# Poisson loss row means: longer load runs, a split first load, and partial sums folded into the last product

## The chip, the cores and the metric

The kernel runs on one core of one Trainium2 chip. The metric is the device time of one execution in microseconds (us). The time of the kernel before is the median of 12 runs.

## The reference

Two float32 arrays of 1024 rows by 4096 columns come in, and one number for each row goes out:

```python
batch, dim = 1024, 4096
loss = np.exp(log_input) - target * log_input
return np.mean(loss, axis=-1).astype(np.float32)
```

That is 33.55 MB of input, one exponential, one product and two sums for each element, and 4 KB of output.

## The kernel before

**Layout.** Partition p of the 128 holds the eight consecutive rows 8p to 8p+7 of both inputs. "Row 3" below means one row of 4096 elements on each of the 128 partitions (2 MB). `x` is `log_input`, `t` is `target`. So the work is rows 0 to 7 of x and t.

**Loads.** The list `loads` gives every transfer in order. Rows 0 to 5 come in pairs: x of two rows, then t of the same two rows, 32 KB per partition and 4 MB each. The list `TAIL` gives the rest in thirty-seconds of a row: row 6 of x and of t whole (2 MB each), and row 7 in smaller pieces, x by 24, 6 and 2, t by 12, 12, 5 and 3 thirty-seconds. All loads are issued by SP (SyncE) on one queue, line L114. The first six are moved ahead of the program's first barrier by `before_first_barrier`; nothing precedes them. The buffers `x_buf` and `t_buf` have three slots of two rows. Rows 6 and 7 reuse the slot of rows 0 and 1, so SP waits at L112 and L113, once, until two exponentials and two products are done (`exp_done`, `prod_done`), and then issues the nine loads of rows 6 and 7.

**ScalarE (ACT).** For each piece of x it computes exp into a PSUM scratch tensor, with the sum over the columns going to a column of `parts` (L139; the sum is written by a second instruction, ACTIVATION_READ_ACCUMULATOR). For each of rows 0 to 6 it also runs a small Copy over the row's two partial sums, scaled by 1/4096, whose sum is the row's loss (`join`, L123). The join of row r stands in ScalarE's order just ahead of the exp of row r + 2, for row 5 ahead of the first piece of row 7, and for row 6 after that piece. The last join, over the six partial sums of row 7 known by then, gives `most`.

**VectorE (DVE).** For each piece of t it computes -t*x with a sum over the columns (L169, again two instructions; the second is DVE_READ_ACCUMULATOR2_ANT). The pieces of t follow the loads of t. The last piece gives `rest`, already scaled. One addition of `most` and `rest` (L180) then gives row 7's loss. SP stores `all_loss`, 128 x 8, with one transfer (L185).

[...] Every load has its own semaphore (`landed`), which the engines wait for.

Of the kernel before, what the change touches and what calls it, by code (L numbers as in the profile page):

```python
# [6 lines left out]
ALU = mybir.AluOpType  # L7
F32 = mybir.dt.float32


TAIL = [
    ("x", 32), ("t", 32), ("x", 24), ("t", 12), ("t", 12), ("x", 6), ("t", 5), ("x", 2), ("t", 3),
]


def before_first_barrier(nc, instructions):

    here, first = nc.cur_bb.bb, nc.main_func.blocks[0]
    names = {i.name for i in instructions}
    here.instructions = [i for i in here.instructions if i.name not in names]
    at = next(
        k
        for k, i in enumerate(first.instructions)
        if i.engine == mybir.EngineType.SP and i.opcode == "Drain"
    )
    first.instructions = first.instructions[:at] + instructions + first.instructions[at:]  # L30


def kernel(tc, log_input, target, out):

    nc = tc.nc
    tc.close()
    tc.compile()  # L48

    P = nc.NUM_PARTITIONS  # L50
    n, d = log_input.shape
    nb = n // P
    assert nb * P == n and tuple(target.shape) == (n, d) and nb == 8 and d % 32 == 0
    inv_d = 1.0 / d
    slots = 3
    groups = nb // 2

    x_v = log_input.rearrange("(p b) d -> p (b d)", b=nb)
    t_v = target.rearrange("(p b) d -> p (b d)", b=nb)
    out_v = out.rearrange("(p b) -> p b", b=nb)  # L60


    loads = []
    for g in range(groups - 1):
        loads += [("x", 2 * d * g, 2 * d), ("t", 2 * d * g, 2 * d)]
    at = {"x": 2 * d * (groups - 1), "t": 2 * d * (groups - 1)}
    for what, w in TAIL:
        loads.append((what, at[what], w * d // 32))
        at[what] += w * d // 32
    assert at == {"x": nb * d, "t": nb * d}  # L70


    def work(kind):
        todo = []
        for i, (what, lo, w) in enumerate(loads):
            if what == kind:
                step = min(w, d)
                todo += [(a, step, i) for a in range(lo, lo + w, step)]
        return todo

    x_work, t_work = work("x"), work("t")
    n_whole = nb - 1
    assert all(w == d for _, w, _ in x_work[:n_whole] + t_work[:n_whole])

    x_buf = nc.alloc_sbuf_tensor("x_buf", [P, slots * 2 * d], F32).ap()
    t_buf = nc.alloc_sbuf_tensor("t_buf", [P, slots * 2 * d], F32).ap()
    e_dump = nc.alloc_psum_tensor("e_dump", [P, d], F32).ap()
    n_parts = len(x_work) - n_whole + len(t_work) - n_whole - 1

    parts = nc.alloc_sbuf_tensor("parts", [P, 2 * n_whole + n_parts], F32).ap()  # L90
    join_dump = nc.alloc_sbuf_tensor("join_dump", [P, 2 * n_whole + n_parts], F32).ap()
    most = nc.alloc_sbuf_tensor("most", [P, 1], F32).ap()
    rest = nc.alloc_sbuf_tensor("rest", [P, 1], F32).ap()
    all_loss = nc.alloc_sbuf_tensor("all_loss", [P, nb], F32).ap()

    def in_slot(lo, w):
        lo %= slots * 2 * d
        return slice(lo, lo + w)

    landed = [nc.alloc_semaphore(f"landed{i}") for i in range(len(loads))]  # L100
    exp_done = nc.alloc_semaphore("exp_done")
    prod_done = nc.alloc_semaphore("prod_done")
    join_done = nc.alloc_semaphore("join_done")
    loss_done = nc.alloc_semaphore("loss_done")
    out_done = nc.alloc_semaphore("out_done")


    early = []
    for i, (what, lo, w) in enumerate(loads):
        buf, src = (x_buf, x_v) if what == "x" else (t_buf, t_v)  # L110
        if lo == 2 * d * slots and what == "x":
            nc.sync.wait_ge(exp_done, 2)  # L112
            nc.sync.wait_ge(prod_done, 2)  # L113
        dma = nc.sync.dma_start(out=buf[:, in_slot(lo, w)], in_=src[:, lo : lo + w])  # L114
        dma.then_inc(landed[i], 16)
        if lo + w <= 2 * d * slots:
            early.append(dma.ins)
    before_first_barrier(nc, early)


    def join(first, count, accum, prods):
        nc.scalar.wait_ge(exp_done, exps)
        return nc.scalar.activation(  # L123
            out=join_dump[:, first : first + count],
            in_=parts[:, first : first + count],
            func=ACT_F.Copy,
            scale=inv_d,
            accum_out=accum,
        ).wait_op(prod_done, prods, "sem-ge")

    exps = 0
    for lo, w, i in x_work:
        row, col = lo // d, lo % d
        if row >= 2 and col == 0:
            join(2 * (row - 2), 2, all_loss[:, row - 2 : row - 1], row - 1).then_inc(join_done, 1)
        if col == 0 and row > 0:
            nc.scalar.wait_ge(exp_done, exps)
        k = 2 * row if row < n_whole else 2 * n_whole + exps - n_whole
        nc.scalar.activation(  # L139
            out=e_dump[:, col : col + w],  # L140
            in_=x_buf[:, in_slot(lo, w)],
            func=ACT_F.Exp,
            bias=0.0,
            scale=1.0,
            accum_out=parts[:, k : k + 1],
        ).wait_op(landed[i], 16, "sem-ge").then_inc(exp_done, 1)
        exps += 1
        if row == n_whole and col == 0:
            row -= 1
            join(2 * row, 2, all_loss[:, row : row + 1], row + 1).then_inc(join_done, 1)  # L150
    join(2 * n_whole, n_parts, most, len(t_work) - 1).then_inc(join_done, 1)


    needs = {}
    for lo, w, i in x_work:
        needs[lo + w] = i
    for j, (lo, w, i) in enumerate(t_work):
        row = lo // d
        last = j == len(t_work) - 1
        if last:  # L160
            accum = rest
        elif row < n_whole:
            accum = parts[:, 2 * row + 1 : 2 * row + 2]
        else:
            k = 2 * n_whole + len(x_work) - n_whole + j - n_whole
            accum = parts[:, k : k + 1]
        x_load = next(needs[end] for end in sorted(needs) if end >= lo + w)
        nc.vector.wait_ge(landed[x_load], 16)
        nc.vector.tensor_tensor_reduce(  # L169
            out=t_buf[:, in_slot(lo, w)],  # L170
            in0=t_buf[:, in_slot(lo, w)],
            in1=x_buf[:, in_slot(lo, w)],
            scale=-inv_d if last else -1.0,
            scalar=0.0,
            op0=ALU.mult,
            op1=ALU.add,
            accum_out=accum,
        ).wait_op(landed[i], 16, "sem-ge").then_inc(prod_done, 1)
    nc.vector.wait_ge(join_done, nb)
    nc.vector.tensor_tensor(  # L180
        out=all_loss[:, nb - 1 : nb], in0=most, in1=rest, op=ALU.add
    ).wait_op(prod_done, len(t_work), "sem-ge").then_inc(loss_done, 1)


    nc.sync.dma_start(out=out_v, in_=all_loss).wait_op(loss_done, 1, "sem-ge").then_inc(  # L185
        out_done, 16
    )
    used = landed + [exp_done, prod_done, join_done, loss_done]
    nc.sync.sem_clear(range(used[0].num, out_done.num))
    assert all(used[0].num <= s.num < out_done.num for s in used)  # L190
    nc.sync.wait_ge(out_done, 16).then_inc(out_done, -16)
# [30 lines left out]
```

## Time and profile before

| | |
|---|---|
| median of 12 runs | 84.26 us (84.18 to 84.51) |
| the profiled execution, its own time | 84.21 us |
| its span in the profile | 82.8 us |
| VectorE busy | 35.9 us (43%) |
| ScalarE busy | 33.7 us (41%) |
| DMA packets, bytes | 2304, 33.56 MB |
| product of a whole row (128x4096), VectorE | 4.42 us each, 7 of them |
| exp of a whole row (128x4096), ScalarE | 3.58 us each, 7 of them |

How to read it. The span runs from the first to the last instruction of the profiled execution; its own time includes what lies around it, 1.41 us. Busy time counts work on data; instructions that wait or issue transfers are not counted. A line of the trace in order of time gives start, duration (both us), engine, line of the kernel, operation, output and inputs, and in brackets how long the engine was idle before it and what ended that. A line of the table by stretches gives the stretch, its length, the busy time of VectorE, ScalarE and GpSimd with the number of instructions, the TensorE clock, the DMA share (packets are counted where they begin, so a short stretch can be above 1), and GB/s.

### The profile page before, as it was taken

What the parts mean: (1) busy time and instruction counts of PE and PEld (TensorE: products, weight loads), DVE (VectorE), ACT (ScalarE), POOL (GpSimd) and SP (SyncE); (2) the same over time, 40 slices, a digit from 0 to 9 for tenths busy, and PEclk for the clock granted to TensorE, in tenths of its full rate; (3) what the DMA queues carried; (4) which work ended last, traced back from release to release, by engine and by line L of the source; (5) the groups of instructions that cost most, each with busy time, mean ns of one, the idle gap of its engine ahead of it and who ended that gap; (6) DMA issues with size and microseconds to landing.
All of it is one profiled execution on the core that took longest, in us unless ns stands there. A gap on an engine that the chain in (4) does not pass through costs nothing.

```text
span 82.8 us, 145 instructions
## 1 busy us (share of the span) xinstructions
DVE 35.9 (43%) x23; ACT 33.7 (41%) x37; POOL 0.2 (0%) x4
## 2 busy tenths in 40 slices
DVE  0000000000499970000099991000069995994992
ACT  0050019994001007999000103999300495019371
POOL 0000000000000000000000000000000000000000
DMA  8699979969997996998899699799899999999950
GB/s 253 285 475 507 427 332 507 507 269 491 507 427 332 507 491 285 491 507 380 380 507 475 285 507 507 332 427 507 348 412 420 451 396 437 421 401 416 398 207 2
DMA packets 2304, 33.56 MB, mean 405 GB/s; under 512 B 384, under 2 KB 640, under 8 KB 1152
## 3 DMA queue, kind: packets, MB, share of 16 engines
q1 hardware_dynamic: 2304, 33.56, 95.6%
HBM read 33.55 MB, written 0.00 MB: 405 GB/s over the span
## 4 chain that ended last, share of the span: by engine, by line
DMA 82%; DVE 7%; issue 6%; SPq 3%
DMA t_buf<-in_target_dram 82%; DVE t_buf L169 6%; SPq L114 3%; DVE parts L169 0%; DVE all_loss L180 0%; DVE rest L169 0%; SPq L113 0%
## 5 line engine op out<-in xcount | busy, mean ns | idle before, releaser
L169 DVE CUSTOM_DVE_ANT_0 t_buf<-t_buf,x_buf 128x4096 f32<-128x4096 f32 (+3 forms) x11 | 35.6, 3260 | 45.4 <-DMA t_buf<-in_target_dram 45.2
L139 ACT ACTIVATE e_dump<-x_buf 128x4096 f32<-128x4096 f32 (+3 forms) x10 | 29.0, 2901 | 23.1 <-DMA x_buf<-in_log_input_dram 22.9
L123 ACT ACTIVATE join_dump<-parts 128x2 f32<-128x2 f32 (+1 forms) x8 | 1.6, 204 | 20.2 <-DVE parts L169 19.8
L139 ACT ACT_TABLE_LOAD x1 | 1.3, 1283 | 4.0 <-PEq L48 4.0
L139 ACT ACTIVATION_READ_ACCUMULATOR e_dump<-x_buf 128x1 f32 x10 | 1.9, 186 | 0.0
L123 ACT ACTIVATION_READ_ACCUMULATOR join_dump<-parts 128x1 f32 x8 | 1.5, 186 | 0.0
L169 DVE DVE_READ_ACCUMULATOR2_ANT parts<- 128x1 f32 x10 | 0.8, 82 | 0.0
L180 DVE TENSOR_TENSOR all_loss<-most,rest 128x1 f32<-128x1 f32 x1 | 0.2, 159 | 0.0
L206 POOL MEMSET const-bfloat16-1.0<- 128x1 bf16 x1 | 0.1, 102 | 0.0
L206 POOL MEMSET const-uint8-127<- 128x1 uint8 x1 | 0.1, 102 | 0.0
L206 POOL MEMSET const-float32-0.0<- 128x1 f32 x1 | 0.1, 99 | 0.2 <-issue 0.2
L206 POOL MEMSET const-float32-1.0<- 128x1 f32 x1 | 0.1, 99 | 0.0
L169 DVE DVE_READ_ACCUMULATOR2_ANT rest<- 128x1 f32 x1 | 0.1, 84 | 0.0
## 6 DMA issues: line engine op xcount, KB each, us to landing
x_buf<-in_log_input_dram SPq DMA_DIRECT2D x3, 4096.0 KB, 30.6
t_buf<-in_target_dram SPq DMA_DIRECT2D x3, 4096.0 KB, 39.8
x_buf<-in_log_input_dram SPq DMA_DIRECT2D x1, 2048.0 KB, 34.9
t_buf<-in_target_dram SPq DMA_DIRECT2D x1, 2048.0 KB, 39.4
x_buf<-in_log_input_dram SPq DMA_DIRECT2D x1, 1536.0 KB, 42.6
t_buf<-in_target_dram SPq DMA_DIRECT2D x2, 768.0 KB, 44.7
x_buf<-in_log_input_dram SPq DMA_DIRECT2D x1, 384.0 KB, 45.9
t_buf<-in_target_dram SPq DMA_DIRECT2D x1, 320.0 KB, 46.3
```

Source lines behind the costliest of these rows:

```text
L114: dma = nc.sync.dma_start(out=buf[:, in_slot(lo, w)], in_=src[:, lo : lo + w])
L123: return nc.scalar.activation(out=join_dump[:, first : first + count], in_=parts[:, first : first + count], func=ACT_F.Copy, scale=inv_d, ...
L139: nc.scalar.activation(out=e_dump[:, col : col + w], in_=x_buf[:, in_slot(lo, w)], func=ACT_F.Exp, bias=0.0, scale=1.0, accum_out=parts[:, ...
L169: nc.vector.tensor_tensor_reduce(out=t_buf[:, in_slot(lo, w)], in0=t_buf[:, in_slot(lo, w)], in1=x_buf[:, in_slot(lo, w)], scale=-inv_d if ...
L180: nc.vector.tensor_tensor(out=all_loss[:, nb - 1 : nb], in0=most, in1=rest, op=ALU.add).wait_op(prod_done, len(t_work), "sem-ge").then_inc ...
L206: nc = _bacc.Bacc("TRN2", target_bir_lowering=False, num_devices=1)
```

## The change

**Buffers and loads.** In place of three slots there is a tensor for four rows (`x_big`, `t_big`, each with six more columns behind the fourth row) and one for two rows (`x_mid`, `t_mid`). The loads become: rows 0 to 3 of x, then of t, 64 KB per partition and 8 MB each; rows 4 and 5 of x, then of t, 32 KB per partition; row 6 of x, then of t; and row 7 in the same pieces as before. The very first load is issued as two transfers on the same semaphore: 16 partitions, then 112. Row 6 goes to the place of row 0, row 7 to the place of row 3, so that the six columns lie right behind row 7's last piece. SP waits twice: for one exp and one product ahead of row 6, for four of each ahead of row 7.

**The end.** The six partial sums of row 7 are written into the columns behind t's last piece; GpSimd writes -1.0 into the columns behind x's last piece. The last product runs over 384 + 6 columns and gives row 7's loss at once. The last join on ScalarE and the addition on VectorE are gone. The last product waits for one semaphore, `last_ready`, which the last load raises by 16, the last exp by 1 and the product before by 1; and for `ones_done`, and for the earlier exps and products. SP waits for the seven joins itself before the store.

```diff
-    ("x", 32), ("t", 32), ("x", 24), ("t", 12), ("t", 12), ("x", 6), ("t", 5), ("x", 2), ("t", 3),
+TAIL = [("x", 24), ("t", 12), ("t", 12), ("x", 6), ("t", 5), ("x", 2), ("t", 3)]
+FIRST = 16
...
-    for g in range(groups - 1):
-        loads += [("x", 2 * d * g, 2 * d), ("t", 2 * d * g, 2 * d)]
-    at = {"x": 2 * d * (groups - 1), "t": 2 * d * (groups - 1)}
+    for first, rows in ((0, 4), (4, 2), (6, 1)):
+        loads += [("x", first * d, rows * d), ("t", first * d, rows * d)]
+    at = {"x": last_row * d, "t": last_row * d}
...
-    x_buf = nc.alloc_sbuf_tensor("x_buf", [P, slots * 2 * d], F32).ap()
-    t_buf = nc.alloc_sbuf_tensor("t_buf", [P, slots * 2 * d], F32).ap()
+    big = {
+        "x": nc.alloc_sbuf_tensor("x_big", [P, 4 * d + n_parts], F32).ap(),
+        "t": nc.alloc_sbuf_tensor("t_big", [P, 4 * d + n_parts], F32).ap(),
+    }
+    mid = {
+        "x": nc.alloc_sbuf_tensor("x_mid", [P, 2 * d], F32).ap(),
+        "t": nc.alloc_sbuf_tensor("t_mid", [P, 2 * d], F32).ap(),
+    }
+    def place(what, lo, w):
+        row = lo // d
+        if 4 <= row < 6:
+            return mid[what][:, lo - 4 * d : lo - 4 * d + w]
+        if row >= 6:
+            lo -= (6 if row == 6 else 4) * d
+        return big[what][:, lo : lo + w]
+    def part(k):
+        return big["t"][:, 4 * d + k : 4 * d + k + 1]
...
-        if lo == 2 * d * slots and what == "x":
-            nc.sync.wait_ge(exp_done, 2)
-            nc.sync.wait_ge(prod_done, 2)
-        dma = nc.sync.dma_start(out=buf[:, in_slot(lo, w)], in_=src[:, lo : lo + w])
-        dma.then_inc(landed[i], 16)
-        if lo + w <= 2 * d * slots:
-            early.append(dma.ins)
+        if what == "x" and lo in (6 * d, 7 * d):
+            free = 1 if lo == 6 * d else 4
+            nc.sync.wait_ge(exp_done, free)
+            nc.sync.wait_ge(prod_done, free)
+        src = x_v if what == "x" else t_v
+        cuts = [0, FIRST, P] if i == 0 else [0, P]
+        sem = landed[i] if i < len(loads) - 1 else last_ready
+        for a, b in zip(cuts, cuts[1:]):
+            dma = nc.sync.dma_start(out=place(what, lo, w)[a:b], in_=src[a:b, lo : lo + w])
+            dma.then_inc(sem, 16)
+            if lo < 6 * d:
+                early.append(dma.ins)
...
+    nc.gpsimd.memset(big["x"][:, 4 * d : 4 * d + n_parts], -1.0).then_inc(ones_done, 1)
...
-    join(2 * n_whole, n_parts, most, len(t_work) - 1).then_inc(join_done, 1)
...
+        if j == 0 or x_load > t_work[j - 1][2]:
+            nc.vector.wait_ge(landed[x_load], full[x_load])
...
+            nc.vector.wait_ge(ones_done, 1)
+            nc.vector.wait_ge(exp_done, n_x - 1)
+            nc.vector.wait_ge(prod_done, n_t - 2)
+            nc.vector.tensor_tensor_reduce(
+                out=place("t", lo, w + n_parts),
+                in0=place("t", lo, w + n_parts),
+                in1=place("x", lo, w + n_parts),
+                scale=-inv_d,
...
+                accum_out=all_loss[:, last_row : last_row + 1],
+            ).wait_op(last_ready, 18, "sem-ge").then_inc(loss_done, 1)
...
-    nc.vector.wait_ge(join_done, nb)
-    nc.vector.tensor_tensor(
-        out=all_loss[:, nb - 1 : nb], in0=most, in1=rest, op=ALU.add
-    ).wait_op(prod_done, len(t_work), "sem-ge").then_inc(loss_done, 1)
+    nc.sync.wait_ge(join_done, last_row)
```

## Prediction

> **What bounds the kernel now.** I read four views of the profile before: the page's chain, the trace's order of time on VectorE and around the end, and the trace cut in short stretches at the start. The page first:
>
> ```profile
> DMA packets 2304, 33.56 MB, mean 405 GB/s; under 512 B 384, under 2 KB 640, under 8 KB 1152
> ...
> q1 hardware_dynamic: 2304, 33.56, 95.6%
> ...
> DMA 82%; DVE 7%; issue 6%; SPq 3%
> ```
>
> The 16 DMA engines are busy for 95.6% of the span, and the chain that ended last is 82% transfer. VectorE (43%) and ScalarE (41%) are spectators until the last microseconds. The next view shows how regular the stream is; each line is a product that starts when its targets have landed:
>
> ```profile
> 21.79 4.42 DVE L169 CUSTOM_DVE_ANT_0 t_buf<-t_buf,x_buf 128x4096 f32<-128x4096 f32 x1 [21.79 <-DMA t_buf<-in_target_dram]
> ...
> 41.23 4.42 DVE L169 CUSTOM_DVE_ANT_0 t_buf<-t_buf,x_buf 128x4096 f32<-128x4096 f32 x1 [10.66 <-DMA t_buf<-in_target_dram]
> ...
> 60.65 4.42 DVE L169 CUSTOM_DVE_ANT_0 t_buf<-t_buf,x_buf 128x4096 f32<-128x4096 f32 x1 [10.64 <-DMA t_buf<-in_target_dram]
> ...
> 70.44 4.42 DVE L169 CUSTOM_DVE_ANT_0 t_buf<-t_buf,x_buf 128x4096 f32<-128x4096 f32 x1 [1.01 <-DMA t_buf<-in_target_dram]
> ```
>
> 8.39 MB land every 19.43 us (432 GB/s), with VectorE idle over 10 us ahead of each pair of rows. The end is another regime:
>
> ```profile
> 79.73 0.82 DVE L169 CUSTOM_DVE_ANT_0 t_buf<-t_buf,x_buf 128x640 f32<-128x640 f32 x1
> 80.09 0.39 ACT L139 ACTIVATE e_dump<-x_buf 128x256 f32<-128x256 f32 x1 [0.27 <-DMA x_buf<-in_log_input_dram]
> 80.41 0.18 ACT L139 ACTIVATION_READ_ACCUMULATOR e_dump<-x_buf 128x1 f32 x1
> 80.48 0.08 DVE L169 DVE_READ_ACCUMULATOR2_ANT parts<- 128x1 f32 x1
> 80.56 0.56 DVE L169 CUSTOM_DVE_ANT_0 t_buf<-t_buf,x_buf 128x384 f32<-128x384 f32 x1
> 80.69 0.21 ACT L123 ACTIVATE join_dump<-parts 128x6 f32<-128x6 f32 x1
> 80.80 0.19 ACT L123 ACTIVATION_READ_ACCUMULATOR join_dump<-parts 128x1 f32 x1
> 81.05 0.08 DVE L169 DVE_READ_ACCUMULATOR2_ANT rest<- 128x1 f32 x1
> 81.16 0.16 DVE L180 TENSOR_TENSOR all_loss<-most,rest 128x1 f32<-128x1 f32 x1
> 81.35 0.35 SPq L185 DMA_DIRECT2D out_dram<-all_loss  x1
> ```
>
> From 79.73 the transfer of 640 columns has landed and VectorE is the path: two products, an addition, then the store. The start, by packets that began in each stretch (last columns: DMA share, GB/s):
>
> ```profile
> 0.80:1.20 0.40, 0.00 (x0) 0.00 (x0) 0.00 (x0) 1.00 2.36 655
> 1.20:1.60 0.40, 0.00 (x0) 0.00 (x0) 0.00 (x0) 1.00 1.55 492
> 1.60:2.00 0.40, 0.00 (x0) 0.00 (x0) 0.00 (x0) 1.00 0.41 164
> 2.00:2.80 0.80, 0.00 (x0) 0.00 (x0) 0.00 (x0) 1.00 0.00 0
> 2.80:3.20 0.40, 0.00 (x0) 0.00 (x0) 0.00 (x0) 1.00 2.89 1229
> 3.20:3.60 0.40, 0.00 (x0) 0.00 (x0) 0.00 (x0) 1.00 0.19 82
> ```
>
> 655 GB/s times 0.4 us is 262 KB, eight packets of 32 KB; then six, then two. So the 16 engines begin their first packet over some 0.75 us (the packet records: 1.02 to 1.76), and their second within 0.38 us. That spread is kept while the stream is steady, and the last engine sets when a load has landed.
>
> [...] The trace has such a wait: the addition of L180 starts 0.03 us after the accumulator read at 81.05 ends.
>
> **The change, part by part.** All sums are against the profiled execution: span 82.80, time 84.21 us (1.41 around the span), which lies 0.05 under the median of 84.26.
>
> (a) Fewer packets. Before, the page's 2304 are 16 DMAs x 16 completion packets (256) and 2048 of data. After, rows 0 to 3 take 256 packets of 64 KB in place of 512 of 32 KB, and there is one load DMA less: 2304 - 256 - 16 = 2032. Price per packet: 4 MB in 32 KB packets (eight per engine) take 9.71 us, and the two 2 MB loads of row 6 (sixteen per engine) take 70.44 - 60.65 = 9.79; 0.08 / 8 is 10 ns. The packet records alone give less: 1.2095 us from one 32 KB packet to the next, 0.607 at best for 16 KB, so 2 x 0.607 - 1.2095 = 5 ns. Each engine saves 16 data packets and one completion: -0.08 to -0.17. I take **-0.10**.
>
> (b) The first load goes out as 16 rows and then 112. SP's first issue lasts 0.37 us for 128 rows[...]. With one row per engine I expect all engines to begin within 0.2 us. The gain is smaller than the spread: the early starters' first packets took 1.8 to 2.0 us, the late ones 1.3 to 1.4 (32 KB, packet records), so all wait for something common, and only the 0.38 us that remain after it are to be had. Nobody can gain more than 0.4; an added issue of 0.4 between first and second part could lose 0.2 if an engine runs dry. I take half of the remaining spread: **-0.20**, ends -0.4 and +0.2.
>
> (c) Later landings in the middle. The first x load now lands when 8 MB are in, at about 21.8 less (a) and (b), the first t load at 41.2: VectorE has nothing for 41 us. Then rows 0 to 3 take 4 x 4.35 = 17.4, to 58.6, while the targets of rows 4 and 5 land at 60.65: 2.0 us of cover. From there the rows meet the same landings as before. ScalarE: row 0's sum waits for the product until 45.7, rows 1 to 3 follow VectorE, row 5's exp ends near 63, the join of row 4 at 65.4, and x of row 6 lands at 65.5 as before. Cost **0**; if the cover went (products 0.5 us slower each), the excess would come back at row 6, where VectorE has another second idle.
>
> (d) SP's waits. Before, one wait ended at 30.6 and nine loads were queued behind it. Now the two loads of row 6 wait for row 0's product (45.7) and the seven loads of row 7 for row 3's (58.7); nothing but loads and the store is behind them on SP. Seven issues of 0.43 to 0.47 end at about 62. The engines have work queued till row 6 ends at 70.4, so each has over 8 us in hand. Before, the late issues blocked for 7.8 to 8.4 us each in SP; that was hidden and goes away unpaid. Cost **0**. POOL's added memset of 128x6 is about 0.1 us, as the page's memsets, and needed 80 us later: 0.
>
> (e) The end. Removed: ScalarE's join (0.21 + 0.19, beside VectorE's product, so worth nothing) and the addition with its gap, 81.13 to 81.35: -0.19 when a hop of 0.03 to SP is left. Added: six columns, (824 - 558) / 256 = 1.04 ns each: +0.006. Added: the last product waits for the earlier product's accumulator (80.56 + 0.03) and for the last exp's, which ends at 80.59. The hop from ScalarE to VectorE is not in the trace at this place: from VectorE to ScalarE it was 0.04 (26.22 to 26.26), from ScalarE to itself 0.10 (80.59 to 80.69). So the start moves from 80.56 to 80.63 to 80.69, +0.07 to +0.13. The other waits ahead of it count things done by 80.1 and pass while VectorE works on 640 columns. Sum -0.11 to -0.05; nothing can hang behind this product but the store. I take **-0.07**.
>
> Sum -0.10 - 0.20 - 0.07 = -0.37: 83.84 for the profiled execution, and with 0.05 up to the median, **83.9 us**.
>
> **The rivals.**
> - *The first 16 rows[...]* (slower). [...] It decides as soon as the 16 rows take over 0.4 us more than their 2.4. [...] I give each of the two conditions four in ten: 0.17.
> - *The start gives nothing* (no change). [...] Then (b) is 0 to +0.2 and the sum -0.17 to +0.03: 84.1 to 84.3. Chance 0.15.
> - *A 64 KB run is cut in two packets*, so the change does not do what it says: (a) shrinks to one completion, the rest stays: 84.0. Within the main case.
> - *A small loss*: (b) at its bad end with a slow hop in (e), above 84.4: 0.06.
>
> **How the numbers follow.** Main case 0.62 with 83.9 (its own range 83.4 to 84.1), no change 0.15, small loss 0.06, ports 0.17. About 0.2% (0.17 us) is what a measurement can tell here from no change. The range 83.4 to 84.7 holds the first three cases and leaves out the ports' 0.17. Faster 0.62, same 0.15, slower 0.06 + 0.17 = 0.23.
>
> **What would show it.** After, the page should have 2032 packets (2288 if a run is cut in two); the first stretch 0.8 to 1.2 nearly all 16 first packets; ScalarE's first exp at about 21.5 and VectorE's first product near 41; VectorE without idle from there to 58.4 and a last product of 390 columns starting about 0.1 after the accumulator read before it, with the store behind it. A first exp beyond 25 us would prove me wrong through the ports; a stream that idles after 60 us, through SP's waits; a last product later than 0.15 behind that read, through the hop.

## The result and the profile after

The changed kernel takes 105.95 us (median; 105.66 to 106.09) against 84.27 us, a ratio of 1.2564 with a 95% interval of 1.2548 to 1.258: 21.7 us slower. (Here and below a ratio follows the means of the runs, so it can differ a little from that of the medians.) It is the first rival of the prediction that came true, far beyond the range of 83.4 to 84.7. The profiled execution's span is 104.5 us.

The page of the changed kernel, in the parts shown of the kernel before:

```profile
GB/s 401 0 0 401 0 401 0 401 351 50 401 276 125 301 100 351 376 426 401 401 401 401 426 401 401 439 489 426 414 414 414 389 426 464 398 405 412 401 153 2
DMA packets 2032, 33.56 MB, mean 321 GB/s; under 512 B 368, under 2 KB 624, under 8 KB 1136
...
q1 hardware_dynamic: 2032, 33.56, 95.3%
```

The 2032 packets are as counted, so the 64 KB runs are single packets (the packet records hold 256 of 65536 bytes). The share of 95.3% is as high as before (95.6%), and yet the mean rate fell from 405 to 321 GB/s: the DMA engines are as busy and move less. The rate by slices says when. Slices are 2.6 us, and bytes are put down to the slice in which a packet begins; in the first eight, slices of 401 stand among empty ones, then the rate rises and falls, and from the sixteenth on it settles near 400. The loss lies in the first 40 us.

The order of time shows the same from the engines' side:

```profile
43.82 3.59 ACT L163 ACTIVATE e_dump<-x_big 128x4096 f32<-128x4096 f32 x1 [38.98 <-DMA x_big<-in_log_input_dram]
...
63.18 4.43 DVE L183 CUSTOM_DVE_ANT_0 t_big<-t_big,x_big 128x4096 f32<-128x4096 f32 x1 [63.18 <-DMA t_big<-in_target_dram]
...
82.61 4.42 DVE L183 CUSTOM_DVE_ANT_0 t_mid<-t_mid,x_mid 128x4096 f32<-128x4096 f32 x1 [1.96 <-DMA t_mid<-in_target_dram]
...
101.58 0.82 DVE L183 CUSTOM_DVE_ANT_0 t_big<-t_big,x_big 128x640 f32<-128x640 f32 x1
102.33 0.08 DVE L183 DVE_READ_ACCUMULATOR2_ANT t_big<- 128x1 f32 x1
102.45 0.57 DVE L201 CUSTOM_DVE_ANT_0 t_big<-t_big,x_big 128x390 f32<-128x390 f32 x1
103.05 0.35 SPq L214 DMA_DIRECT2D out_dram<-all_loss  x1
```

x of rows 0 to 3, forecast for about 21.5, is complete at 43.8. From there everything runs at the old pace: 19.4 us to the first product (8.39 MB), 19.4 to that of rows 4 and 5. Rows 0 to 3 of x are the only load that was cut, and they are 22 us late.

The start, in the stretches shown of before:

```profile
0.80:1.20 0.40, 0.00 (x0) 0.00 (x0) 0.00 (x0) 1.00 12.16 1475
1.20:1.60 0.40, 0.00 (x0) 0.00 (x0) 0.00 (x0) 1.00 6.64 819
1.60:2.00 0.40, 0.00 (x0) 0.00 (x0) 0.00 (x0) 1.00 2.56 328
2.00:8.80 6.80, 0.00 (x0) 1.28 (x1) 0.10 (x1) 1.00 0.00 0
```

At 64 KB a packet these are nine, five and two first packets, nearly the eight, six and two of before: one row per engine did not bring the engines' starts together. From 2.0 to 8.8 us no packet begins: all sixteen engines are still at their first one. The DMA share tells the rest. It counts a packet's whole duration in the stretch where it begins: 12.16 x 0.4 us x 16 engines over nine packets is 8.6 us each. A packet of the same size in t of rows 0 to 3 takes 2.42 us. That is from the packet records, the trace's list of single packets with start and duration; they also give 7.9 to 9.3 us for each of the first sixteen (8.5 on average; all of them together last from 1.00 to 10.38 us), and 2.9 to 5.8 for the 112 that follow (9.02 to 42.85 us).

### The profile page after: what moved, and what is told of

The parts are those of the page before. It is cut to its first block, busy times and chain, and to the rows that moved or that the text cites. A ratio compares the mean times of both kernels' runs of the same rounds, so it can differ in the third digit from the quotient of the medians.

```text
span 104.5 us, 132 instructions
## 1 busy us (share of the span) xinstructions
DVE 35.6 (34%) x22; ACT 33.2 (32%) x35; POOL 0.3 (0%) x5
## 2 busy tenths in 40 slices
DMA packets 2032, 33.56 MB, mean 321 GB/s; under 512 B 368, under 2 KB 624, under 8 KB 1136
## 3 DMA queue, kind: packets, MB, share of 16 engines
q1 hardware_dynamic: 2032, 33.56, 95.3%
## 4 chain that ended last, share of the span: by engine, by line
DMA 60%; another core or an unknown queue 18%; DVE 14%; issue 4%; SPq 2%; DVEq 0%
DMA x_big<-in_log_input_dram 60%; DVE t_big L183 14%; SPq L137 2%; DVE t_big L201 1%; DVE parts L183 0%; DVEq L200 0%; DVEq L181 0%; SPq L132 0%; DVE all_loss L201 0%
## 5 line engine op out<-in xcount | busy, mean ns | idle before, releaser
L183 DVE CUSTOM_DVE_ANT_0 t_big<-t_big,x_big 128x4096 f32<-128x4096 f32 (+2 forms) x8 | 26.2, 3307 | 65.4 <-DMA t_big<-in_target_dram 65.3
L163 ACT ACTIVATE e_dump<-x_big 128x4096 f32<-128x4096 f32 (+3 forms) x8 | 21.8, 2729 | 45.2 <-DMA x_big<-in_log_input_dram 44.8
L183 DVE CUSTOM_DVE_ANT_0 t_mid<-t_mid,x_mid 128x4096 f32<-128x4096 f32 x2 | 8.8, 4422 | 2.0 <-DMA t_mid<-in_target_dram 2.0
L149 ACT ACTIVATE join_dump<-parts 128x2 f32<-128x2 f32 x7 | 1.4, 203 | 20.5 <-DVE parts L183 20.4
L163 ACT ACTIVATE e_dump<-x_mid 128x4096 f32<-128x4096 f32 x2 | 7.1, 3568 | 0.0
L163 ACT ACTIVATION_READ_ACCUMULATOR e_dump<-x_big 128x1 f32 x8 | 1.5, 187 | 0.0
L201 DVE CUSTOM_DVE_ANT_0 t_big<-t_big,x_big 128x390 f32<-128x390 f32 x1 | 0.6, 566 | 0.0
## 6 DMA issues: line engine op xcount, KB each, us to landing
t_big<-in_target_dram SPq DMA_DIRECT2D x1, 2048.0 KB, 24.3
```

The lines of the kernel that those rows point to most:

```text
L149: nc.scalar.activation(out=join_dump[:, 2 * row : 2 * row + 2], in_=parts[:, 2 * row : 2 * row + 2], func=ACT_F.Copy, scale=inv_d, accum_o ...
L163: nc.scalar.activation(out=e_dump[:, col : col + w], in_=place("x", lo, w), func=ACT_F.Exp, bias=0.0, scale=1.0, accum_out=parts[:, 2 * ro ...
L183: nc.vector.tensor_tensor_reduce(out=place("t", lo, w), in0=place("t", lo, w), in1=place("x", lo, w), scale=-1.0, scalar=0.0, op0=ALU.mult ...
L201: nc.vector.tensor_tensor_reduce(out=place("t", lo, w + n_parts), in0=place("t", lo, w + n_parts), in1=place("x", lo, w + n_parts), scale= ...
```

## The experiments

**Theories.** Theory 1: cut by partitions, the rows of a piece slow each other by where in SBUF they go, in proportion to bytes; the runs below test which places are slow. Theory 2: runs of 64 KB, or the late landings that they bring, cost the time. Theory 3: two transfers for one load at the head of the queue cost it, however they are cut. The edits below are shown by their main lines; the counts that waits expect, and with the old end also the buffers, change to match.

### The first load in one piece, with the new end and with the old

```diff
-        cuts = [0, FIRST, P] if i == 0 else [0, P]
+        cuts = [0, P]
```

> The changed kernel with the first x load in one piece of 128 partitions; all else as changed. Theory 1[...]: the whole loss of 21.7 us goes, the first exp starts at about 21.7 us, and 83.8 to 84.1 us are left, from the packets (-0.10) and the end (-0.07 to -0.26). Theory 2 (runs of 64 KB or the late landings cost the time): it stays above 100 us.

Measured: 84.01 us against 84.20, ratio 0.9978 (0.9964 to 0.9991). The whole loss is gone; theory 2 falls. Three lines of its order of time confirm the middle of the prediction:

```profile
21.83 3.59 ACT L163 ACTIVATE e_dump<-x_big 128x4096 f32<-128x4096 f32 x1 [17.60 <-DMA x_big<-in_log_input_dram]
...
41.17 4.43 DVE L183 CUSTOM_DVE_ANT_0 t_big<-t_big,x_big 128x4096 f32<-128x4096 f32 x1 [41.17 <-DMA t_big<-in_target_dram]
...
60.60 4.43 DVE L183 CUSTOM_DVE_ANT_0 t_mid<-t_mid,x_mid 128x4096 f32<-128x4096 f32 x1 [1.96 <-DMA t_mid<-in_target_dram]
```

VectorE does nothing for 41 us, catches up, and waits 1.96 us for rows 4 and 5; the cover was put at 2.0.

The second kernel takes the loads alone, with ScalarE's last join and the addition kept:

```diff
-    for g in range(groups - 1):
-        loads += [("x", 2 * d * g, 2 * d), ("t", 2 * d * g, 2 * d)]
+    for first, rows in ((0, 4), (4, 2), (6, 1)):
+        loads += [("x", first * d, rows * d), ("t", first * d, rows * d)]
```

> The kernel before with the new loads and buffers (rows 0 to 3 in one run of 64 KB, first load in one piece) and its own end: ScalarE's last join and VectorE's addition stay. Theory 1: the loads alone are worth -0.1 (fewer packets), 84.1 to 84.2, and this lies 0.05 to 0.2 above the run with the new end. Theory 2: above 100 us.

Measured: 84.28 us against 84.20, ratio 1.0002 (0.9986 to 1.0017), a little above what was expected. The long runs as such change nothing that can be measured (in the profiled executions row 6's product starts at 70.38 in place of 70.44). The medians put this kernel 0.27 us above the one with the new end, but the two intervals still touch; that the gain is with the end rests on the traces. From the start of the product of 640 columns to the store it was 1.62 us before (79.73 to 81.35), and it is 1.62 here, where the old end is kept:

```profile
79.66 0.82 DVE L179 CUSTOM_DVE_ANT_0 t_big<-t_big,x_big 128x640 f32<-128x640 f32 x1
...
81.28 0.35 SPq L195 DMA_DIRECT2D out_dram<-all_loss  x1
```

With the new end, in the one-piece kernel, it is 1.51:

```profile
79.70 0.83 DVE L183 CUSTOM_DVE_ANT_0 t_big<-t_big,x_big 128x640 f32<-128x640 f32 x1
80.07 0.39 ACT L163 ACTIVATE e_dump<-x_big 128x256 f32<-128x256 f32 x1 [0.27 <-DMA x_big<-in_log_input_dram]
80.39 0.19 ACT L163 ACTIVATION_READ_ACCUMULATOR e_dump<-x_big 128x1 f32 x1
80.45 0.08 DVE L183 DVE_READ_ACCUMULATOR2_ANT t_big<- 128x1 f32 x1
80.61 0.56 DVE L201 CUSTOM_DVE_ANT_0 t_big<-t_big,x_big 128x390 f32<-128x390 f32 x1
81.10 0.08 DVE L201 DVE_READ_ACCUMULATOR2_ANT all_loss<- 128x1 f32 x1
81.21 0.35 SPq L214 DMA_DIRECT2D out_dram<-all_loss  x1
```

The last product starts at 80.61: 0.08 after VectorE's own accumulator read, and 0.03 after ScalarE's ends at 80.58. The last product thus starts right behind ScalarE's sum of the last exp, for which it did not have to wait before.

### The cut alone, in the kernel before

```diff
-        dma = nc.sync.dma_start(out=buf[:, in_slot(lo, w)], in_=src[:, lo : lo + w])
+        cuts = [0, 16, P] if i == 0 else [0, P]
+        for a, b in zip(cuts, cuts[1:]):
+            dma = nc.sync.dma_start(out=buf[a:b, in_slot(lo, w)], in_=src[a:b, lo : lo + w])
```

> The kernel before with one edit: its first x load (rows 0 and 1, 32 KB per partition) goes out as 16 partitions and then 112. Theory 1: the cost goes with the bytes that the split load moves, half of those in the changed kernel, so 11 us: about 95. Theory 2 (64 KB runs or late landings at fault): no change, 84.3. Theory 3 (a fixed cost of two transfers on one semaphore at the head of the queue): the same 21.7 us, 106.

Measured (two runs): 93.85 us, ratio 1.1138 (1.1094 to 1.1181), 9.6 us more. The cut alone does it, and with half the bytes it costs a little under half (21.9 between the changed kernel and the one-piece one). A fixed cost would have given 106.

### The cut turned by 90 degrees

```diff
-        cuts = [0, FIRST, P] if i == 0 else [0, P]
+        cuts = [0, 2048, w] if i == 0 else [0, w]
...
-            dma = nc.sync.dma_start(out=place(what, lo, w)[a:b], in_=src[a:b, lo : lo + w])
+            dma = nc.sync.dma_start(out=place(what, lo, w)[:, a:b], in_=src[:, lo + a : lo + b])
```

> The changed kernel with the first load cut by columns in place of partitions: 128 partitions x 2048 columns (8 KB runs), then 128 x 14336 (56 KB runs), both on the same semaphore. Theory 1:[...] nothing is lost but 8 packets and a completion per engine, some 0.05 to 0.1: 83.9 to 84.2. Theory 3 (two transfers at the head cost it): about 106.

Measured: 83.84 us, ratio 0.9966 (0.9933 to 1.0). Two transfers at the head, on one semaphore, cost nothing when each spans all 128 partitions: theory 3 falls.

### The loads by themselves

This kernel computes nothing; SP issues one load, waits for it, and issues the next. It was run once.

> The loads alone, one after the other with a wait between them, 64 KB per partition, no loss computed (the output is zeros): 128 partitions; 16 neighbours from 16 neighbouring rows of HBM; 16 partitions four apart from the same rows; 16 neighbours from rows four apart; 8 neighbours; 8 four apart; partitions 64 to 127; 16 to 127; 0 to 31. Theory 1[...]: about 2 us of latency and 19.3; 9.6; 4.8; 9.6; 9.6; 2.4; 19.3[...] 30 or so, as in the changed kernel; 9.6[...] If the HBM side were at fault, the third would be as slow as the second and the fourth faster. If an engine's own rate were the only limit, 16 rows and 8 rows would take 2.4 wherever they lie.

The order of time, where each load is issued once the load in the line above has landed; lines 32, 34, 36 and so on follow the list in the expectation:

```profile
1.55 0.40 SPq L30 DMA_DIRECT2D a_all<-in_log_input_dram  x1
23.37 0.35 SPq L32 DMA_DIRECT2D b_16near<-in_log_input_dram  x1
34.86 0.57 SPq L34 DMA_DIRECT2D a_all<-in_log_input_dram  x1
42.45 0.33 SPq L36 DMA_DIRECT2D b_16near<-in_target_dram  x1
54.12 0.32 SPq L38 DMA_DIRECT2D a_all<-in_target_dram  x1
65.43 0.70 SPq L40 DMA_DIRECT2D b_16near<-in_target_dram  x1
70.53 0.52 SPq L42 DMA_DIRECT2D a_all<-in_target_dram  x1
93.20 0.34 SPq L44 DMA_DIRECT2D b_16near<-in_log_input_dram  x1
127.79 0.32 SPq L46 DMA_DIRECT2D a_all<-in_target_dram  x1
140.29 0.37 SPq L48 DMA_DIRECT2D out_dram<-loss  x1
```

| load, 64 KB per partition | from issue to next issue, us |
|---|---|
| partitions 0 to 127 | 21.8 |
| 0 to 15, from 16 neighbouring rows of HBM | 11.5 |
| 0, 4, ... 60, from the same rows | 7.6 |
| 0 to 15, from rows four apart | 11.7 |
| 0 to 7 | 11.3 |
| 0, 4, ... 28 | 5.1 |
| 64 to 127 | 22.7 |
| 16 to 127 | 34.6 |
| 0 to 31 | 12.5 |

The times include about 2.4 us of latency: 128 partitions take 21.8 here and 19.4 in the stream. The forecast for theory 1, an estimate of the author's ahead of about 2 us of latency, has every large difference right. The measured times lie 1.7 to 3.4 us above it; only partitions 16 to 127, put at "30 or so", lie 4.6 above. Eight rows take 11.3 us side by side and 5.1 us four apart: the same bytes, the same number of packets, only another place. Moving the source rows in HBM changes nothing (11.5 and 11.7). And 64 rows in the upper half take longer than all 128. What decides is where in SBUF the rows go: neighbours slow each other (11.3 us for partitions 0 to 7), while 0, 4, ... 28 take 5.1, little more than one packet of 2.42 and the latency, and 0, 4, ... 60 take 7.6. Why these places differ was not shown; the traces hold the times of packets and nothing of their way into SBUF.

A second kernel of this kind, also run once, at 32 KB per partition, asked whether it is the number of rows or their place:

> Loads alone again, one after the other with a wait between them, 32 KB per partition, nothing computed (zeros as output): partitions 32 to 95, 0 to 63, 0 to 127, 0 to 111, 16 to 111, 0 to 119, 0 to 95, 32 to 79. A packet alone takes 1.21 us, and latency adds about 2.2. Theory 1[...]: 0 to 63[...] 64 rows at half speed, 12; 32 to 95[...] 7; 0 to 127 as known, 12; 0 to 111 half of what 64 KB took for 112 rows, 18 to 19. If the number of rows and not their place were what matters, 32 to 95 and 0 to 63 would take the same. 0 to 119[...] 20. The others have no forecast beyond at least 7.3 + 2.2 for 96 rows and 3.6 + 2.2 for 48.

```profile
1.55 0.61 SPq L31 DMA_DIRECT2D a_all<-in_log_input_dram  x1
9.08 0.50 SPq L33 DMA_DIRECT2D b_16near<-in_log_input_dram  x1
21.74 0.35 SPq L35 DMA_DIRECT2D a_all<-in_target_dram  x1
33.74 0.34 SPq L37 DMA_DIRECT2D b_16near<-in_target_dram  x1
50.54 0.32 SPq L39 DMA_DIRECT2D a_all<-in_log_input_dram  x1
```

Partitions 32 to 95 take 7.5 us, 0 to 63 take 12.7, all 128 take 12.0, and 0 to 111 take 16.8. Less 2.4 of latency, 64 rows' worth of bytes takes 5.1 us or 10.3, by place alone. What sets 0 to 63 apart from 32 to 95 was not shown. For 112 rows the forecast was too high (18 to 19). The other counts were slow too: 96 rows 16.2 (from partition 16) and 16.6 (from 0), 48 rows 9.4, 120 rows 22.2, where 20 had been put.

### Other cuts in the changed kernel

```diff
-FIRST = 16
+FIRST = 64
```

> The changed kernel with the first load cut at partition 64 in place of 16. [...] The probe's packets of 64 KB took 5.12 us there in place of 2.42, so x of rows 0 to 3 takes 8 x 5.12 = 41.0 in place of 19.4 us: 21.6 more than in one piece, 105.6. If it were the small first part that costs (16 rows at 9 us), a cut in the middle would cost clearly less than the changed kernel's 21.9.

```diff
-        cuts = [0, FIRST, P] if i == 0 else [0, P]
+        pieces = [(32, 96), (0, 32), (96, P)] if i == 0 else [(0, P)]
```

> The changed kernel with the first load in three pieces: partitions 32 to 95, then 0 to 31, then 96 to 127. By the probes the first piece[...] (4 x 2.42 = 9.7 us), the other two[...] (2 x 5.12 each): 30.2 in place of 19.4, 10.8 more than in one piece, 94.8. If the number of transfers or the split as such cost the time, three pieces would be no cheaper than two: 105 or more.

Measured (two runs each): 105.32 us (ratio 1.2491, 1.2407 to 1.2576) for the cut at 64, and 95.09 us (1.1279, 1.1202 to 1.1355) for three pieces; 105.6 and 94.8 were expected. Stretches of the cut at 64, then of the three pieces (last column GB/s):

```profile
0.00:10.00 10.00, 0.00 (x0) 1.28 (x1) 0.31 (x5) 1.00 0.99 210
10.00:20.00 10.00, 0.00 (x0) 0.00 (x0) 0.00 (x0) 1.00 1.02 210
20.00:30.00 10.00, 0.00 (x0) 0.00 (x0) 0.00 (x0) 1.00 1.01 210
30.00:40.00 10.00, 0.00 (x0) 0.00 (x0) 0.00 (x0) 1.00 1.02 210
```

```profile
0.00:10.00 10.00, 0.00 (x0) 1.28 (x1) 0.30 (x5) 1.00 1.03 419
10.00:20.00 10.00, 0.00 (x0) 0.00 (x0) 0.00 (x0) 1.00 0.97 210
20.00:30.00 10.00, 0.00 (x0) 0.00 (x0) 0.00 (x0) 1.00 1.00 210
30.00:40.00 10.00, 0.00 (x0) 6.77 (x3) 0.00 (x0) 1.00 1.01 419
```

The engines are busy all the time in both (share 0.97 to 1.03). The stretches go at 210 or at 419 GB/s: 210 for both pieces of the cut at 64 and for partitions 0 to 31 and 96 to 127, 419 for partitions 32 to 95 and again once t comes with all 128. Three pieces cost less than two, so the number of transfers is not it.

### Is there a gain in the start at all?

The cut by columns once more, at 512 columns, and alone in the kernel before:

> The kernel with the cut at 2048 columns once more, for its interval: 83.8 to 83.9, a ratio of 0.995 to 0.997 to the kernel before, as the sum of the end (-0.11) and the start (-0.2).

> The changed kernel with the first load cut by columns at 512 (2 KB runs first) in place of 2048. If the cut helps because the engines' first packets are short, 2 KB does at least as well as 8 KB: 83.7 to 83.85. If the first part is over[...] before the second part's descriptors are there, some engines run dry and 0.1 to 0.3 is lost: 83.9 to 84.1.

> The kernel before with one edit: its first x load is cut by columns, 128 partitions x 2048, then x 6144. In the changed kernel such a cut brought the first exp from 21.83 to 21.61 us. If that is the start of the engines (short first packets close up the spread of their starts) and has nothing to do with runs of 64 KB: 0.15 to 0.2 less than before, 84.0 to 84.05. If it depends on the long runs: 84.2 as before.

Measured: cut at 2048 again 83.98 us, ratio 0.9968 (0.9958 to 0.9979); at 512 83.94, ratio 0.9954 (0.9937 to 0.9971); in the kernel before 84.28 against 84.25, ratio 0.9997 (0.9986 to 1.0008). The last shows no gain, so the expected 0.15 to 0.2 from the start is refuted for that kernel. The repeat lies in the expected range by its ratio and just above it by its median; its first exp came at 21.73 us, where the first run of the same kernel had 21.61 and the one-piece kernel 21.83, so half of that start gain did not come again. The run at 512 columns lies in the range of its second forecast, but it is no slower than the cut at 2048, so the loss that this forecast was built on does not show. In the changed kernel the cut stands 0.001 to 0.0024 of the time (0.1 to 0.2 us) below the one-piece kernel's 0.9978, and the intervals overlap: not settled. The versions with the cut by columns are faster than both kernels all the same, by 0.3 to 0.5% against the kernel before (in the first of the three runs the interval reaches 1.0).

## Why the prediction was wrong

- **The step that failed is (b)**, the first load as 16 rows and then 112. It was to bring -0.20 and brought +21.9 (105.95 against 84.01 without the cut). Two assumptions were in it. That one row per engine lets all engines begin within 0.2 us: they began over 0.80 us (1.00 to 1.80), as before (0.74). And that the 16 and 112 rows move at the speed of a load of 128, 432 GB/s: they moved at 112 (1.05 MB from 1.00 to 10.38 us) and 217 GB/s (7.34 MB from 9.02 to 42.85).
- **The case was on record as a rival, with too low a chance.** "Ports" in the prediction is its name for the case that the first 16 rows, each on a DMA engine of its own, slow each other by where in SBUF they go; no run shows a port. Both of these conditions, given four in ten each, hold. Sixteen packets, one per row, were in flight together (all had begun by 1.80 us, none had ended by 9.0); and each took 7.9 to 9.3 us for its 64 KB in place of 2.42. The sign named for this rival, a first exp beyond 25 us, is there at 43.82. The 0.17 was the author's estimate: the trace of before has loads of 128 partitions alone and shows nothing of smaller ones. The loads by themselves give the answer: 1.05 MB into partitions 0 to 15 took 11.5 us (91 GB/s, latency included), where 8.39 MB into all 128 took 21.8.
- **The price follows from the loads by themselves.** 11.5 us for the 16 rows and 34.6 for the 112, less 21.8 for the load of 128, is 24.3. One latency of 2.4 in this does not count, since the two parts follow each other without a wait in the changed kernel: 21.9 (an estimate from these runs). The changed kernel's x is 22.0 late against one piece (43.82 - 21.83).
- **(a) fewer packets**: the count of 2032 was right, the price not measurable: -0.10 forecast, ratio 1.0002 with an interval of 0.0015 either way.
- **(c) and (d), the late landings and SP's waits**: right. VectorE waited 1.96 us for rows 4 and 5, and SP issued the last seven loads at 58.74 to 61.95 in the one-piece kernel, 8 us ahead of need. In the changed kernel it is the same shifted by 22 us.
- **(e) the end**: right in kind, at the better bound: -0.11 in the profiled execution where -0.07 was taken. The hop from ScalarE to VectorE, put at 0.04 to 0.10, is 0.03.

Without step (b) the forecast would have been -0.17, and the one-piece kernel came out 0.19 faster by its medians (0.08 to 0.30 by the interval). That the two agree is partly luck: -0.10 of the forecast was for fewer packets, which gave nothing that could be measured, and the end gave -0.11 in the trace where -0.07 was taken. Where the rest of the 0.19 comes from is not shown.

## What to carry to other kernels

Before cutting a load, ask which partitions each piece covers: pieces of all 128 partitions (cut along the columns) kept the full rate in every run here (8.39 MB in 19.4 us). Pieces of fewer neighbouring partitions ran slower, down to half or a quarter of it (210 and 112 GB/s where 419 was possible), partitions 32 to 95 alone excepted, and everything behind them on the queue came late by that much. A DMA share near 100% does not mean full speed (95.3% came with 321 GB/s here, 95.6% with 405); read GB/s by stretches beside it. And where a step's price hangs on a transfer that the trace does not have, measure that transfer by itself first: here one load of 16 rows, 11.5 us.

## What the runs showed of the hardware that I had not expected

- Partitions 32 to 95 load at full speed (32 KB each in 7.5 us with latency), 0 to 63 at half (12.7 us, longer than all 128 in 12.0). "Fewer than 128 is slow" is too simple; the place decides.
- A packet of 64 KB takes 5.12 us (median) when partitions 64 to 127 are loaded, 6% more than twice the 2.42 of a load of all 128. With partitions 0 to 15 alone it takes 8.5 on average, 3.5 times 2.42.
- 112 rows were slow as well: 33.8 us for their packets in the changed kernel, with a median of 4.65 us for a packet in place of 2.42. So were 96 rows: 16.2 and 16.6 us at 32 KB per partition, where all 128 took 12.0. How rows of these counts are dealt out to the engines was not shown.
